# Hybrid encoder trunk on one core: last part of the down projection in written order, merge units reordered, second multiplier transposed later

## The chip, the core and the metric

The kernel runs on one core of a Trainium2 chip. The metric is device time in microseconds for the whole program, both layers. PE is TensorE's matmul stream, PEld its weight loads, DVE is VectorE, ACT is ScalarE, POOL is GpSimd; SP issues most of the DMAs.

## The reference, cut to what matters

A trunk of two layers on 256 positions by 1024 channels, all in float32. Each layer is

```
h = rmsnorm(x, norm1_g) * (1 + sc1) + sh1
x = x + g1 * token_mix(h)          # Fourier branch and retention branch, merged by gates
h = rmsnorm(x, norm2_g) * (1 + sc2) + sh2
x = x + g2 * conv_ffn(h)           # up projection, conv, gelu gate, down projection
```

and a last rmsnorm follows. The six vectors sh, sc, g come from one conditioning vector times `ada_w` (1024 x 6144 in each layer). In `token_mix` the two branch results are merged as `sigmoid(a_f) * y_f + sigmoid(a_r) * y_r`, where a_f and a_r are projections of h, y_f is the Fourier branch times `w_fourier` and y_r is the retention branch times `w_ret`.

## The kernel before, in words

**Precision by splitting.** Each float32 operand is held as a high part and a remainder: `split` (L60) has ACT write the rounded copy (L61) and DVE the difference (L62). Each product is then three matmuls: high by high, and the two mixed ones (`mm_xs` L138, `mm_ws` L144).

**Weights.** `plan` (L75 to L96) lists all weight blocks of 1 MB in the order of use. `ahead` loads a block into one of four `raw` buffers by SP and splits it into two halves, each in a `wt` buffer (four of them, so two blocks) or, for some, in a general buffer (`wb`). `nextw` takes the next block and prepares the one after. A buffer is free again only when its last reader is done, so a load on SP or a split on ACT may wait for that.

**Conditioning.** `ada_dots` (L194) loads 1 MB of `ada_w` into a `raw` buffer and makes two dot products on DVE (L184). They fill gaps: `side` issues a few in each stage, and `pl` says which. A finished multiplier column (`gc`) is turned into a row by a PE transpose, an ACT copy and two DMAs from POOL's queue (`rows`, L214 to L221).

**Order.** The code is traced in the order written; a scheduler then sets the order on every engine by its own estimate of what is ready first, and each engine runs its list in that order. `later(n, fn)` and `tick` (L123, L126) place a small piece of work n steps further on in the trace.

**Merge** (L588 to L622). Four column blocks c; for each, four units of 48 matmuls (`mm_w`): z = 0 and 1 are the gate projections of h (tile `hT`), z = 2 the Fourier branch (`yf`), z = 3 the retention branch (`yrT`). The last head's attention runs among the units of c = 0, and its normed result is transposed (L598) and split into the second half of `yrT`, which the unit z = 3 of c = 0 reads.

**FFN.** After the output projection and the second norm come 22 tiles of the up projection (three of them in another layout, their transposes at L686), each with convolution and gate. The down projection keeps four accumulators, two row blocks m of 128 positions by two column blocks z of 512 (in the last layer the second row block has columns of 512, 256 and 256), and walks through 11 weight blocks. For the first 7 it does all four accumulators at each block; the last SK = 4 blocks (`ws`: two in `wt`, two in `wb`) are all prepared first, and then each accumulator is finished in turn (L725 to L732). After each column follow the residual (rt L735, c_xs L736), and squares for the next norm (L738); `norm_mod` (L268) then makes 1/rms on POOL (L232), scales (xn, L242 on DVE and L244 on ACT), and a few ticks later transposes (L251) and modulates (hm, L262 and L264) and splits into `hT`, which the first projection of the next layer reads.

## Time and profile before

| what | value |
|---|---|
| median of 3 runs | 897.24 us (893.81 to 897.34) |
| profiled execution, its own time | 897.42 us |
| its span, first to last instruction | 895.6 us |
| PE busy, matmuls | 98%, 6250 |
| DVE busy, ACT busy | 82%, 56% |
| mean granted TensorE clock | 0.992 |
| bytes by DMA, mean rate | 210.85 MB, 235 GB/s |

Busy shares are means over the whole span; busy PE is modelled from the size of each matmul, so that matmuls in a row overlap. What matters here is where PE's list stands still, and on which instruction of another engine. The profiled execution lies 0.18 us above the median of the runs, and 1.86 us of its time lie outside the span.

### The profile page before, as it was taken

To read this page: it belongs to the slowest core of one execution; us is meant where nothing else is said; L and a number is where in the kernel's file an instruction comes from. 1 tells how busy PE (TensorE), PEld (TensorE's weight loads), DVE (VectorE), ACT (ScalarE), POOL (GpSimd) and SP (SyncE) were. 2 spreads that over 40 slices of the span, in tenths; PEclk is the share of its full clock that TensorE was granted. 3 is DMA by queue.
4 is the path that set the end of the run, shared out by engine and by line. 5 is a ranking of instruction groups with operands and counts; after the bars stand their busy time and mean duration, and the time that the engine had idled before them with its cause. 6 is when DMAs were issued, how large, how long until landed. Compare 5 with 4: busy or idle time off the path is not lost.

```text
span 895.6 us, 15358 instructions
## 1 busy us (share of the span) xinstructions
PE 874.5 (98%) x6250; PEld 816.1 (91%) x6250; DVE 735.7 (82%) x1135; ACT 500.7 (56%) x736; POOL 23.0 (3%) x33
## 2 busy tenths in 40 slices
PE   7999999899999999999989999999999999999996
PEld 5889999899989999998878899999998999999885
DVE  6899999788885999899687879997777769999563
ACT  5666446344465876763474545554444767677441
POOL 1000000000000000000000000010000000000000
PEclk9999999999999999999999999999999999999999
DMA  8995665878884356579755666657778444655521
GB/s 322 378 348 201 236 236 194 300 295 299 311 336 145 142 190 209 199 257 407 291 188 188 249 245 223 253 194 261 280 272 324 171 165 165 210 207 195 188 95 48
DMA packets 33033, 210.85 MB, mean 235 GB/s; under 512 B 4001, under 2 KB 4289, under 8 KB 10178
## 3 DMA queue, kind: packets, MB, share of 16 engines
q1 hardware_dynamic: 31682, 207.16, 63.3%
q0 software_dynamic: 704, 2.11, 0.7%
q8 instruction: 49, 0.80, 0.3%
q10 hardware_dynamic: 576, 0.59, 0.2%
q14 instruction: 22, 0.18, 0.1%
HBM read 208.79 MB, written 1.06 MB: 234 GB/s over the span
## 4 chain that ended last, share of the span: by engine, by line
PE 83%; DVE 9%; DMA 3%; issue 2%; ACT 2%; POOL 1%; POOLq 0%; SPq 0%; ACTq 0%
PE ps L148 48%; PE ps L141 11%; PE ps L140 11%; PE ps L142 11%; DVE wt L62 3%; DMA raw<-in_ada_dram 2%; DVE raw L184 2%; PE ps L251 1%; DMA raw<-in_wx_dram 1%; PE ps L463 1%; DVE qk L62 1%; ACT wt L61 1%; DVE rc L501 0%; DVE rsn L502 0%; DVE yrT L62 0%
## 5 line engine op out<-in xcount | busy, mean ns | idle before, releaser
L148 PE MATMUL ps<-hT,wt 128*128 128x256 f32 x3368 | 392.1, 277 | 0.0
L148 PEld LDWEIGHTS ps<-hT,wt 128*128 128x128 f32 x3368 | 388.2, 188 | 0.4
L62 DVE TENSOR_TENSOR wt<-raw,wt 128x1024 fp32r<-128x1024 f32 (+1 forms) x270 | 325.8, 1214 | 72.3 <-ACT wt L61 70.8
L61 ACT ACTIVATE wt<-raw 128x1024 fp32r<-128x1024 f32 (+1 forms) x270 | 282.2, 1052 | 175.8 <-PE ps L148 84.5
L184 DVE CUSTOM_DVE_ANT_0 raw<-raw,c_cbc,c_adab 128x1024 f32<-128x1024 f32 x96 | 121.2, 1280 | 9.7 <-DMA raw<-in_ada_dram 9.5
L140 PE MATMUL ps<-wt,hT 128*128 128x512 f32 (+1 forms) x240 | 84.1, 367 | 4.8 <-ACT hT L61 2.5
L141 PE MATMUL ps<-wt,hT 128*128 128x512 f32 (+1 forms) x240 | 87.8, 366 | 0.0
L142 PE MATMUL ps<-wt,hT 128*128 128x512 f32 (+1 forms) x240 | 87.8, 367 | 0.0
L647 ACT ACTIVATE cv<-ps,c_cvw 128x256 f32<-128x256 f32 x88 | 49.4, 561 | 29.6 <-PE ps L148 17.9
L141 PE MATMUL ps<-wt,act 128*128 128x512 f32 (+1 forms) x162 | 59.3, 367 | 0.0
L142 PE MATMUL ps<-wt,act 128*128 128x512 f32 (+1 forms) x162 | 59.2, 366 | 0.0
L140 PE MATMUL ps<-wt,act 128*128 128x512 f32 (+1 forms) x162 | 58.7, 366 | 0.0
L140 PEld LDWEIGHTS ps<-wt,hT 128*128 128x128 f32 x240 | 45.4, 190 | 13.3 <-ACT hT L61 3.4
L142 PEld LDWEIGHTS ps<-wt,hT 128*128 128x128 f32 x240 | 46.1, 192 | 7.6
L141 PEld LDWEIGHTS ps<-wt,hT 128*128 128x128 f32 x240 | 46.0, 192 | 6.9
L148 PE MATMUL ps<-yrT,wt 128*128 128x256 f32 x384 | 49.0, 288 | 3.0 <-DVE yrT L62 3.0
L148 PEld LDWEIGHTS ps<-yrT,wt 128*128 128x128 f32 x384 | 47.5, 195 | 3.5 <-DVE yrT L62 3.3
L148 PE MATMUL ps<-yf,wt 128*128 128x256 f32 x384 | 46.5, 281 | 0.0
L648 DVE SCALAR_TENSOR_TENSOR cv<-ps,c_cvw,cv 128x255 f32<-128x255 f32 x88 | 41.1, 479 | 6.3 <-ACT cv L647 6.1
L148 PEld LDWEIGHTS ps<-yf,wt 128*128 128x128 f32 x384 | 45.8, 189 | 0.0
L651 DVE SCALAR_TENSOR_TENSOR cv<-ps,c_cvw,cv 128x255 f32<-128x255 f32 x88 | 41.2, 480 | 1.6
L141 PEld LDWEIGHTS ps<-wt,act 128*128 128x128 f32 x162 | 30.6, 189 | 5.2 <-DVE wt L62 0.3
(154 smaller groups left out, 940.5 us busy)
## 6 DMA issues: line engine op xcount, KB each, us to landing
raw<-in_ww_dram SPq DMA_DIRECT2D x48, 1024.0 KB, 5.5
raw<-in_ada_dram SPq DMA_DIRECT2D x40, 1024.0 KB, 4.9
raw<-in_up_dram SPq DMA_DIRECT2D x38, 1024.0 KB, 4.8
raw<-in_wx_dram SPq DMA_DIRECT2D x24, 1024.0 KB, 6.6
raw<-in_down_dram SPq DMA_DIRECT2D x22, 1024.0 KB, 4.8
raw<-in_ada_dram SPq DMA_DIRECT2D x16, 512.0 KB, 7.4
raw<-in_wx_dram SPq DMA_DIRECT2D x16, 512.0 KB, 6.9
raw<-in_upx_dram SPq DMA_DIRECT2D x6, 1024.0 KB, 7.3
```

The lines of the kernel that those rows point to most:

```text
L61: A.activation(dst_h, src if hi_src is None else hi_src, AF.Copy)
L62: V.tensor_tensor(out=dst_l, in0=src, in1=dst_h.bitcast(F32), op=ALU.subtract)
L140: T.matmul(pt, xh, wh, start=start, stop=False)
L141: T.matmul(pt, xh, wl, start=False, stop=False)
L142: T.matmul(pt, xl, wh, start=False, stop=stop)
L148: T.matmul(pt[:, z], w, x[:, z], start=start and i == 0, stop=stop and i == 2)
L184: V.tensor_tensor_reduce(out=wb, in0=wb, in1=cbc, scale=1.0, scalar=adab[:, l, v * KT + k : v * KT + k + 1], op0=ALU.mult, op1=ALU.add, ac ...
L251: T.transpose(pt[:, b * P : (b + 1) * P], xn[:, b * P : (b + 1) * P], ident)
L463: T.matmul(pt, dfc[:, x, part, :], pq[i][:, y, :, o : o + P], start=(j == 0), stop=(j == 2))
L647: A.activation(o, pt, AF.Identity, scale=cvw[:, l, 1, c : c + 1], bias=cvw[:, l, 3, c : c + 1])
L648: V.scalar_tensor_tensor(out=o[:, 1:], in0=pt[:, : S - 1], scalar=cvw[:, l, 0, c : c + 1], in1=o[:, 1:], op0=ALU.mult, op1=ALU.add)
L651: V.scalar_tensor_tensor(out=o[:, : S - 1], in0=pt[:, 1:], scalar=cvw[:, l, 2, c : c + 1], in1=o[:, : S - 1], op0=ALU.mult, op1=ALU.add)
```

## The change

Four edits:

1. **Merge.** The 16 units are named by a table `MERGE` of (c, z). The unit z = 3 of c = 0, the first reader of `yrT`, now comes after (1, 0), the first gate projection of the next column block. The plan of weights follows the table. The conditioning loads of a column block are still issued after its unit z = 3, so they are traced one unit later for c = 0.
2. **Down projection, last part.** PE follows the written order from the last four weight blocks on to the end of the loop (`manual_schedule`). Row block m = 0 is finished before m = 1, and within a row block the weight block is the outer loop and the column the inner one (but for the second row block of the last layer). The norm's transposes come 2 ticks later for m = 0 (after 24 matmuls of m = 1) and 3 for m = 1.
3. **Weight splits behind the modulation.** When the first norm's modulation of m = 0 for the next layer has been traced, weight splits after the first two halves are issued behind its split on ACT and DVE (`hold`, `issue_after`), until the next layer has its first four blocks.
4. **Second multiplier.** `rows` for g2 no longer comes at the end of the merge; it is kept in `behind` and issued after the third transposed FFN tile.

```
+MERGE = [(0, 0), (0, 1), (0, 2), (1, 0), (0, 3), (1, 1), (1, 2), (1, 3)] + [(c, z) for c in (2, 3) for z in range(4)]
...
     def split(dst_h, dst_l, src, hi_src=None):
-        A.activation(dst_h, src if hi_src is None else hi_src, AF.Copy)
-        V.tensor_tensor(out=dst_l, in0=src, in1=dst_h.bitcast(F32), op=ALU.subtract)
+        h = A.activation(dst_h, src if hi_src is None else hi_src, AF.Copy)
+        l = V.tensor_tensor(out=dst_l, in0=src, in1=dst_h.bitcast(F32), op=ALU.subtract)
+        return h.ins, l.ins
...
-        for c in range(4):
-            plan += [(w_[8 + 4 * z + c], 0, 64) for z in range(4)]
+        plan += [(w_[8 + 4 * z + c], 0, 64) for c, z in MERGE]
...
-                split(t[:, 0, :], t[:, 1, :], w[:, c * 1024 : (c + 1) * 1024])
+                with ExitStack() as order:
+                    for ins in hold[1:] if hold and hold[0] <= 0 else ():
+                        order.enter_context(tc.issue_after(ins))
+                    split(t[:, 0, :], t[:, 1, :], w[:, c * 1024 : (c + 1) * 1024])
+                if hold:
+                    hold[0] -= 1
...
-        later(2, rows)
+        if i == 0:
+            later(2, rows)
+        else:
+            behind.append(rows)
...
+        def mod(hf):
+            made = modulate(l, i, m, hf, norm_t(xns[hf]), hp[hf])
+            if i == m == 0:
+                hold[:] = [2, *made]
...
             wu = [nextw(3 - i) for i in range(4)]
+            hold.clear()
...
+        for c, z in MERGE:
+            pt = ps()
+            mm_w(pt, (hp, hp, yfp, yrp)[z], nextw(), 0 if (c, z) == (1, 1) else None)
+            if z < 2:
+                t = sig[c, z] = tmp("sig")
                 A.activation(t, pt, AF.Sigmoid)
+                continue
+            t = sig[c, z - 2]
+            V.tensor_tensor(out=t, in0=pt, in1=t, op=ALU.mult)
+            if z == 2:
+                continue
+            y, t = sig.pop((c, 0)), sig.pop((c, 1))
+            V.tensor_tensor(out=y, in0=y, in1=t, op=ALU.add)
             o = mp[c // 2][:, :, 2 * (c % 2) : 2 * (c % 2) + 2, :]
+            split(o[:, 0], o[:, 1], y.rearrange("p (b t) -> p b t", b=2))
             side("c", (len(pl["c"]) + 3 - c) // (4 - c))
...
         for j in range(NX):
             later(2 * j + 1, lambda j=j: t_gated(j))
+        while behind:
+            later(2 * NX - 1, behind.pop())
...
+        end = ExitStack()
+        end.enter_context(tc.manual_schedule(engines={mybir.EngineType.PE}))
         for m in range(2):
...
+            n = len(cols[m])
+            if m == 1 and last:
+                order = [(i, z) for z in range(n) for i in range(SK)]
+            else:
+                order = [(i, z) for i in range(SK - 1) for z in range(n)] + [(SK - 1, z) for z in range(n)]
+            for x, (i, z) in enumerate(order):
+                for kk in range(2):
+                    down(ws[i], NT - SK + i, m, z, kk)
+                if i == SK - 1:
+                    column(z)
+                if x % 2 == 1:
+                    tick()
...
-                norm_mod(l + 1, 0, m, hp, ss, 3, 3)
+                norm_mod(l + 1, 0, m, hp, ss, 2 + m, 2 + m)
```

What moves on the engines is seen at three places. In all of these rows ps is an accumulator in PSUM; line numbers are those of the kernel they are from, and L148 before is L157 now, L62 is L64, L184 is L193.

PE in the merge of the first layer, before: yf is the Fourier unit of c = 0, gpart holds the retention result, whose transposes are the x8 row.

```order
L148 MATMUL ps<-yf,wt 128x256 x48
L598 MATMUL ps<-c_ident,gpart 128x128 x8
L148 MATMUL ps<-yrT,wt 128x256 x13
L148 MATMUL ps<-hT,wt 128x256
L148 MATMUL ps<-hT,wt 128x128 x3
L148 MATMUL ps<-yrT,wt 128x256 x35
```

and now:

```order
L157 MATMUL ps<-yf,wt 128x256 x48
L613 MATMUL ps<-c_ident,gpart 128x128 x8
L157 MATMUL ps<-hT,wt 128x256 x48
L157 MATMUL ps<-yrT,wt 128x256 x48
L157 MATMUL ps<-hT,wt 128x256
```

A whole gate unit of 48 matmuls now stands between the transposes and the first matmul on `yrT`.

DVE at the same place, now: ag and vr are the statistics of the last head, nb the bias for its norm, the ISA rows with raw are conditioning dot products, sig is the merge's multiply.

```order
L552 BN_AGGR ag<-bs 128x2 x2
L193 ISA raw,sct<-raw,c_cbc,c_adab 128x1024
L193 ISA sct 128x1
L554 TENSOR_SCALAR vr<-ag 128x2
...
L558 SCALAR_TENSOR_TENSOR nb<-ag,rr 128x2
L64 TENSOR_TENSOR wt<-raw,wt 128x1024
L565 TENSOR_TENSOR gpart<-yn,gpart 128x256 x2
...
L632 TENSOR_TENSOR sig<-ps,sig 128x512
L193 ISA raw,c_sh_98<-raw,c_cbc,c_adab 128x1024
L193 ISA c_sh_98 128x1
L64 TENSOR_TENSOR yrT<-ps,yrT 128x4x128 x2
```

Before, these first two dots (sct) stood ahead of the statistics, the c_sh dots around nb and the gc dots ahead of the `yrT` split; each of them now stands one place later. The rows left out are the second sct dot behind vr, and one row of sc and one weight split behind gpart.

DVE at the layer boundary, now, from the first row block's scaled half (xn) on: rt and c_xs are the residual of the second row block, wt and wb weight splits of the next layer's first four blocks.

```order
L254 TENSOR_SCALAR xn<-c_xs,rs 128x512
L64 TENSOR_TENSOR wt<-raw,wt 128x1024 x2
L276 TENSOR_SCALAR hm<-ps,c_sc_103,c_sh_99 128x128 x4
L64 TENSOR_TENSOR hT<-hm,hT 128x4x128 x2
L64 TENSOR_TENSOR wt<-raw,wt 128x1024
L754 TENSOR_TENSOR rt<-ps,g_600 128x512
L64 TENSOR_TENSOR wt<-raw,wt 128x1024
L755 TENSOR_TENSOR c_xs<-c_xs,rt 128x512
L64 TENSOR_TENSOR wb<-raw,wb 128x1024
```

and before:

```order
L242 TENSOR_SCALAR xn<-c_xs,rs 128x512
L735 TENSOR_TENSOR rt<-ps,g_600 128x512
L62 TENSOR_TENSOR wt<-raw,wt 128x1024
L736 TENSOR_TENSOR c_xs<-c_xs,rt 128x512
L62 TENSOR_TENSOR wt<-raw,wt 128x1024 x2
L264 TENSOR_SCALAR hm<-ps,c_sc_103,c_sh_99 128x128 x2
L735 TENSOR_TENSOR rt<-ps,g_600 128x512
L264 TENSOR_SCALAR hm<-ps,c_sc_103,c_sh_99 128x128 x2
L736 TENSOR_TENSOR c_xs<-c_xs,rt 128x512
L62 TENSOR_TENSOR hT<-hm,hT 128x4x128 x2
```

The modulation of the first row block now runs in one piece, ahead of the second block's residual and of all but two weight splits. On PE the transposes that feed it had 12 down-projection matmuls behind them before the first use of `hT`; now they have 24.

More of the change, by code (lines that the diff above doesn't have):

```diff
@@ L121, in trunk @@
     waiting = []
+    behind = []
     def later(n, fn):
@@ L272, in norm_mod @@
         for hf, t in ((0, t0), (1, t1)):
-            later(t, lambda hf=hf: modulate(l, i, m, hf, norm_t(xns[hf]), hp[hf]))
+            later(t, lambda hf=hf: mod(hf))
     def tok(m):
@@ new lines, in trunk, with yr_t, last_scores @@
+        yrp = [pair("yrT", [4, S]) for i in range(2)]
+        def yr_t(hf):
+            for m in range(2):
+                pt = ps()
+                for b in range(4):
+                    T.transpose(pt[:, b * P : (b + 1) * P], yr[:, m, hf * 512 + b * P :][:, :P], ident)
+                split(yrp[hf][:, 0, :, tok(m)], yrp[hf][:, 1, :, tok(m)], pt.rearrange("p (b t) -> p b t", b=4))
+        def last_scores():
+            sts[H - 1] = scores(H - 1, qks.pop(H - 1))
+        later(1, last_scores)
@@ new lines, in trunk @@
+        later(2, lambda: yr_t(0))
+        later(3, lambda: attend(H - 1, sts.pop(H - 1)))
+        later(6, lambda: yr_t(1))
+        sig = {}
+        for c, z in MERGE:
[3 more added lines that the diff above has]
+                t = sig[c, z] = tmp("sig")
+                A.activation(t, pt, AF.Sigmoid)
+                continue
[5 more added lines that the diff above has]
+            V.tensor_tensor(out=y, in0=y, in1=t, op=ALU.add)
@@ L620, in trunk @@
             o = mp[c // 2][:, :, 2 * (c % 2) : 2 * (c % 2) + 2, :]
-            split(o[:, 0], o[:, 1], sig[0].rearrange("p (b t) -> p b t", b=2))
+            split(o[:, 0], o[:, 1], y.rearrange("p (b t) -> p b t", b=2))
             side("c", (len(pl["c"]) + 3 - c) // (4 - c))
@@ L724, in trunk, with column @@
             nc.sync.dma_start(fg, a["rowv"].to_broadcast([P, D]))
+        end = ExitStack()
+        end.enter_context(tc.manual_schedule(engines={mybir.EngineType.PE}))
         for m in range(2):
             ss = sp.tile([P, 4], F32, tag="ss", name="ss", bufs=3)
-            for z, (c0, w) in enumerate(cols[m]):
-                for i in range(SK):
-                    for kk in range(2):
-                        down(ws[i], NT - SK + i, m, z, kk)
-                    if i % 2 == 1:
-                        tick()
+            def column(z):
+                c0, w = cols[m][z]
                 cs = slice(c0, c0 + w)
@@ L756, in trunk @@
                     A.dma_start(out[0, tok(m), s], o)
+        end.close()
 def _tables():
```

29 lines of the change are left out of this document (2 added, 27 removed).

## The prediction

> **What bounds the kernel now.** I read the page first, then PE's waits, then the granted clock in stretches around the longest of them, and last the order of time on PE, DVE, ACT and POOL there.
>
> ```profile
> PE 874.5 (98%) x6250; PEld 816.1 (91%) x6250; DVE 735.7 (82%) x1135; ACT 500.7 (56%) x736; POOL 23.0 (3%) x33
> ...
> PE 83%; DVE 9%; DMA 3%; issue 2%; ACT 2%; POOL 1%; POOLq 0%; SPq 0%; ACTq 0%
> ```
>
> PE is the bound: 98% busy, and 83% of the chain that ended last. No edit changes its 6250 matmuls, so what can be won are the moments in which its list stands still. The view of PE's waits (us in total, times, longest) names them:
>
> ```profile
> PE ps L148 <- DVE yrT L62: 3.0, 2, 2.7
> PE ps L140 <- ACT hT L61: 2.5, 2, 2.3
> PE ps L172 <- DMA c_cbc<-in_crow_dram: 2.5, 1, 2.5
> PE ps L140 <- ACT wt L61: 2.3, 1, 2.3
> ```
>
> The third and fourth are at the start, which the change doesn't touch. The first is the merge unit that reads `yrT` (2.7 us in the first layer, 0.3 in the second); the second is the first matmul of layer 2 on `hT`. Each long stop has a second price. Stretches, with busy us and instructions for PE, PEld, DVE, ACT, POOL, then the granted clock, the DMA share and GB/s:
>
> ```profile
> 165.50:171.50 6.00, 3.36 (x27) 3.02 (x26) 5.45 (x9) 2.03 (x3) 0.00 (x0) 1.00 0.97 310
> 171.50:175.00 3.50, 3.46 (x16) 3.46 (x17) 1.12 (x1) 0.66 (x1) 0.00 (x0) 0.51 0.77 281
> 451.00:454.80 3.80, 1.49 (x7) 0.88 (x6) 3.80 (x9) 3.23 (x8) 0.00 (x0) 1.00 0.84 276
> 454.80:458.30 3.50, 3.50 (x10) 2.73 (x10) 3.06 (x5) 3.38 (x5) 1.46 (x1) 0.51 0.27 56
> ```
>
> Right behind each stop the clock is 0.51 for 3.5 us, so 3.5 x 0.49 = 1.7 us more are lost.
>
> [...]
>
> **Merge, first layer.** PE in order of time:
>
> ```profile
> 166.34 1.94 PE L148 MATMUL ps<-yrT,wt 128*128 128x256 f32 x13
> 168.12 0.75 PE L148 MATMUL ps<-hT,wt 128*128 128x256 f32 x4
> 171.54 5.83 PE L148 MATMUL ps<-yrT,wt 128*128 128x256 f32 x35 [2.68 <-DVE yrT L62]
> 177.21 11.23 PE L148 MATMUL ps<-hT,wt 128*128 128x128 f32 x94
> 188.28 5.82 PE L148 MATMUL ps<-yf,wt 128*128 128x256 f32 x48
> 193.93 5.82 PE L148 MATMUL ps<-yrT,wt 128*128 128x256 f32 x48
> ```
>
> From 188.28 to 193.93 a unit of 48 takes 5.65 us, 0.118 each. From 166.34 to 177.21 are 13 + 4 + 35 = 52 matmuls: 6.12 us at that pace, 10.87 taken, so **4.75 us lost** (the stop, the slow clock, and 0.3 of small ones). What was late stands on DVE and POOL:
>
> ```profile
> 158.69 0.76 DVE L533 BATCH_NORM_STATS2 bs<-ps 128x6 f32<-128x256 f32 x2
> 160.02 1.61 POOL L538 TENSOR_TENSOR rr<-vr,c_nhalf 128x2 f32<-128x2 f32 x1 [3.38 <-DVE vr L536]
> 164.08 0.76 DVE L547 TENSOR_TENSOR gpart<-yn,gpart 128x256 f32<-128x256 f32 x2
> 166.05 1.29 DVE L184 CUSTOM_DVE_ANT_0 raw<-raw,c_cbc,c_adab 128x1024 f32<-128x1024 f32 x1 [1.22 <-DMA raw<-in_ada_dram]
> 170.21 1.28 DVE L62 TENSOR_TENSOR yrT<-ps,yrT 128x512 fp32r<-128x512 f32 x2
> ...
> 154.91 0.33 SPq L67 DMA_DIRECT2D raw<-in_ada_dram  x1
> ...
> 157.31 8.72 DMA raw<-in_ada_dram
> ...
> raw<-in_ada_dram SPq DMA_DIRECT2D x40, 1024.0 KB, 4.9
> ```
>
> DVE runs its list in order, and a conditioning dot whose load took 8.72 us (median of its kind 4.9) stood ahead of the split. Now unit (1, 0) runs from 166.34 to 172.0, and the unit on `yrT` reads the second half's remainder after 13 more matmuls, at 173.5. Unchanged, the split would end at 171.5. But the dots move too. The loads are traced one unit later, so the load issued at 154.91, second of three, is now the first; at 4.9 us it lands at 159.8. Its first dot now stands ahead of vr, whose statistics end at 159.7: vr at 161.1 (dot 1.29), POOL 1.61, then the bias, ACT's norm and the two gpart multiplies, about 2 us together: 164.8, just what the two multiplies reach now (164.08 + 0.76 = 164.84), because the other dot ran ahead of the weight split there. The second load, issued when the first one's buffer comes free (two dots, 162.3), lands at 167.2, its dot ends at 168.5, and the two splits at 169.8: 3.7 us ahead of need. Gain 4.75, bounds 0 (as late as before, or a new stop of the same price) and 4.75. I take 4.6. The weights of (1, 0) and (0, 3) only swap places in the same four `wt` buffers.
>
> **Merge, second layer.**
>
> ```profile
> 605.45 1.94 PE L148 MATMUL ps<-yrT,wt 128*128 128x256 f32 x13
> 607.23 0.96 PE L148 MATMUL ps<-hT,wt 128*128 128x256 f32 x7
> 608.49 4.39 PE L148 MATMUL ps<-yrT,wt 128*128 128x256 f32 x35 [0.30 <-DVE yrT L62]
> 612.72 10.88 PE L148 MATMUL ps<-hT,wt 128*128 128x256 f32 x91
> ```
>
> 55 matmuls take 7.27 us against 55 x 0.118 = 6.47: **0.8 us lost**, no slow clock. The need moves back by 5.65 us, and ahead of the split stand as many dots as before, two. Gain 0.8, bounds 0 and 0.8.
>
> **Layer boundary.**
>
> ```profile
> 430.03 0.39 PE L140 MATMUL ps<-wt,act 128*128 128x512 f32 x1
> ...
> 443.36 0.68 DVE L735 TENSOR_TENSOR rt<-ps,g 128x512 f32<-128x512 f32 x1
> 446.89 0.71 ACT L244 ACTIVATE xn<-c_xs,rs 128x512 f32<-128x512 f32 x1
> 447.72 1.03 PE L251 MATMUL ps<-c_ident,xn 128*128 128x128 f32 x8
> 451.10 0.39 PE L142 MATMUL ps<-wb,act 128*128 128x512 f32 x1
> 451.44 0.73 DVE L264 TENSOR_SCALAR hm<-ps,c_sc,c_sh 128x128 f32<-128x128 f32 x2
> 453.80 0.50 PE L140 MATMUL ps<-wt,hT 128*128 128x512 f32 x1 [2.31 <-ACT hT L61]
> 453.91 1.30 DVE L62 TENSOR_TENSOR hT<-hm,hT 128x512 fp32r<-128x512 f32 x2
> 455.41 1.46 POOL L232 TENSOR_TENSOR rs<-ss,c_nhalf 128x1 f32<-128x1 f32 x1 [9.01 <-DVE ss L230]
> 458.95 0.39 PE L140 MATMUL ps<-wt,hT 128*128 128x512 f32 x1
> ...
> L62 DVE TENSOR_TENSOR wt<-raw,wt 128x1024 fp32r<-128x1024 f32 (+1 forms) x270 | 325.8, 1214 | 72.3 <-ACT wt L61 70.8
> ```
>
> From 430.03 to 447.72 are 78 matmuls, 0.227 each. The last down matmul starts at 451.10 and is through at 451.33; 15 matmuls on `hT` follow up to 458.95, which need 3.4 us and take 7.62: **4.2 us lost**. The cause is the order: transposes at 447.72, with only 12 matmuls (2.7 us) behind them.
>
> The new order ends the last down matmul at the same 451.33, since the matmuls are the same. Row block 1 then fills 48 x 0.227 + 0.8 of transposes = 11.7 us, so row block 0 is through at 439.6, and its transposes stand after 24 matmuls, at 445.1. From the second column's rt to the end of xn the trace takes 443.36 to 447.60 = 4.2 us; from 439.9 that gives 444.1, so PE doesn't stop at the transposes (1.0 us to spare). They end at 445.9. The modulation and splits then need, in one piece, the four hm and two `hT` rows of DVE (0.7 for a pair, 1.30): by 449, against need at 451.3. If it all took as long as before (447.72 to 453.80, 6.1 us) it would be 451.2, still no stop.
>
> What is late next is row block 1's norm. DVE has, from about 449.0 on, two wt and four wb splits (1.2 each), two rt and two c_xs (0.6 each), ss and xn ahead of the end of that xn: 10.2 us, so 459.2 with ACT and POOL at their short durations, 460.1 with the 1.46 us of POOL above. PE reaches these transposes 36 matmuls (8.2 us) after 451.33, at 459.5. A stop of 0 to 1.0 us; I take 0.5. Each of the six halves of weights held back comes about 2.5 us ahead of its use by the same count. Gain 4.2 - 0.5 = 3.7; bounds 0.2 (a new stop as dear as the old one) and 4.2.
>
> **The rest.** In the last layer's tail PE waits for one weight half once:
>
> ```profile
> 868.02 0.19 PEld L141 LDWEIGHTS ps<-wt,act 128*128 128x128 f32 x1 [0.32 <-DVE wt L62]
> ```
>
> The new order needs that half 6 matmuls later: gain 0.15, bounds 0 and 0.3. The second multiplier's transpose is one matmul on PE wherever it stands; POOL's two DMAs for it now come behind the norm's power instead of ahead of it, and no wait of PE names them: 0. PE would have to stand in front of that transpose for it to cost, and its column is made before the output projection begins.
>
> **Sum.** 4.6 + 0.8 + 3.7 + 0.15 = 9.25 us. The profiled execution took 897.42 (span 895.6 and 1.8 around it), so 888.2; it lies 0.2 above the median of the runs, so I predict **888.0 us**. Own range of this case: 886.0 to 890.5 (up to 2.5 us of new small stops).
>
> **Rivals.**
> - *The merge stop comes back in the first layer.* Now a dot stands ahead of vr. With a load of 8.72 us instead of 4.9, vr, the transposes and all behind them are 3.8 us later; PE stands 3.0 us, plus 1.7 of slow clock: 4.7 us, so 892.7. For it: such a load is in the trace, at this very place. Against it: that load flew beside the multiplier row's broadcast and behind another load, and the one issued at 154.91 landed in time for its dot.
> - *The boundary stop moves to row block 1's transposes.* PE can't pass them, and xn needs 10.2 us of DVE's list behind 449. If the whole list is 2 us later, the stop is 2.5 us and the clock halves: 4.2 instead of 0.5, so 891.7. Against it: 451.2 is the latest the trace gives for `hT`, and DVE then has less in front.
> - *Nothing gained.* Both of the above at once, and no gain in the second layer: 888.0 + 4.7 + 3.7 + 0.8 = 897.2.
> - *Slower.* One mechanism: DVE's list held by the first conditioning load in the merge. Each us that it lands after 160.8 is a us of PE, plus 1.7 in all. To eat the 9.25 us and 4.5 more it must land 12 us after that, an 18 us load: the slowest loads named above took 8.72. Time then from 902 on.
> - *The pieces don't act.* The orders above show that they do; what is unsure is only whether something else was the last to arrive.
>
> **How the numbers follow.** Chances: forecast 0.58, first rival 0.17, second 0.14, nothing gained 0.07, slower 0.04. A change of 0.5%, 4.5 us, is about what a measurement of this kernel can tell from none: below 892.8 is faster. The forecast, the second rival, and half of the first lie there: 0.58 + 0.14 + 0.08 = 0.80; same 0.16; slower 0.04. The range: with all terms at their upper bounds (4.75 + 0.8 + 4.2 + 0.3 = 10.05) the median would be 887.2, and I go 1.4 below that, since one of the three runs before was 3.4 us faster than the other two; above, it takes in both rivals: 885.8 to 893.4.
>
> **What would show it.** Right: PE's waits no longer name `yrT` or the first `hT` with more than 0.5 us; the clock is 1.00 in every stretch after the start; between the transposes of row block 0 and the first `hT` matmul stand 24 down matmuls without idle time; the gpart multiplies end within 1 us of the `yf` unit's end. Wrong: a stretch at 0.51 near 170 or 460; an idle time ahead of L263 (the transposes) above 1 us; a dot with idle time from a DMA ahead of vr. If the time is above 893 though these stops are gone, the lost time has another source than PE's order.

## The result, and the profile after

| | before | changed |
|---|---|---|
| median of the runs side by side (4 each) | 896.38 us (893.81 to 897.34) | 887.57 us (887.22 to 888.77) |
| profiled execution, its span | 897.42, 895.6 us | 888.77, 886.9 us |
| mean granted clock | 0.992 | 0.998 |

The ratio is 0.9904, with a 95% interval of 0.9884 to 0.9924: faster by about 1%. The prediction was 888.0 us. The total came out nearly as forecast; how it came about did not, as the stages below show.

The page of the changed kernel, busy time and the chain that ended last, and its view of PE's waits (us in total, times, longest):

```profile
PE 867.5 (98%) x6250; PEld 809.2 (91%) x6250; DVE 736.7 (83%) x1135; ACT 501.8 (57%) x736; POOL 22.1 (2%) x33
...
PE 75%; DVE 13%; DMA 5%; ACT 3%; issue 3%; POOL 1%; POOLq 0%; SPq 0%; ACTq 0%; DVEq 0%
...
PE ps L149 <- ACT wt L63: 3.9, 2, 2.3
PE ps L150 <- DVE wt L64: 2.3, 2, 1.3
PE ps L149 <- ACT hT L63: 0.2, 1, 0.2
```

The waits on `yrT` and on the first `hT` of layer 2, 2.7 and 2.3 us before, are gone. New are waits on split weights (`wt`): of the first row 1.6 us and of the second all 2.3 us stand at the two output projections. PE's busy time fell by 7.0 us with the same number of matmuls; the two stretches of slow clock, 3.4 us each at a granted clock of 0.50, account for 3.4 of that, and the rest needs another cause. Not all of the waits on weights are new: the second output projection had one of 0.6 us before. And 13% of the chain now run over DVE and 5% over DMA, against 9% and 3%.

**Stages.** From both traces, the time between landmarks on PE: start is the 17th matmul on `hT` (at 19.18 us before and 19.07 now, behind the slow clock of the start: 0.51 from 14.5 to 18.0 us before; matmuls 0.43 us apart up to 16.6 us now, and 0.23 from 17.0 on), T is the second set of transposes ahead of a merge's `yrT` (L598 before, L613 after), W the first matmul of the output projection, N the first transpose of the second norm, F the last transpose of the transposed FFN tiles, D the first down matmul, E the discrete transform of layer 2. In us:

| stage | before | changed | difference | predicted |
|---|---|---|---|---|
| start to T, layer 1 | 146.38 | 146.40 | 0.0 | 0 |
| T to W, merge of layer 1 | 79.28 | 72.27 | -7.0 | -4.6 |
| W to N, output projection | 16.47 | 20.37 | +3.9 | 0 |
| N to D, FFN's up projection | 129.26 | 129.85 | +0.6 | 0 |
| D to E, down projection and boundary | 87.70 | 84.15 | -3.55 | -3.7 |
| E to T, layer 2 | 126.39 | 127.01 | +0.6 | 0 |
| T to W, merge of layer 2 | 75.33 | 71.85 | -3.5 | -0.8 |
| W to N | 17.28 | 17.68 | +0.4 | 0 |
| N to D | 129.26 | 129.75 | +0.5 | 0 |
| D to the end | 69.03 | 68.56 | -0.5 | -0.15 |

The ten differences make -8.5 us. The rows of the FFN's up projection, 129 us long, show how well a stage repeats that no edit means to touch: within 0.6 us.

**The merge of layer 1 went by the prediction's walk.** DVE, POOL and PE of the changed kernel in order of time:

```profile
159.84 1.26 DVE L193 CUSTOM_DVE_ANT_0 raw<-raw,c_cbc,c_adab 128x1024 f32<-128x1024 f32 x1
161.03 0.16 DVE L554 TENSOR_SCALAR vr<-ag 128x2 f32<-128x2 f32 x1
161.34 1.61 POOL L556 TENSOR_TENSOR rr<-vr,c_nhalf 128x2 f32<-128x2 f32 x1 [4.46 <-DVE vr L554]
164.20 0.75 DVE L565 TENSOR_TENSOR gpart<-yn,gpart 128x256 f32<-128x256 f32 x2
167.48 1.28 DVE L193 CUSTOM_DVE_ANT_0 raw<-raw,c_cbc,c_adab 128x1024 f32<-128x1024 f32 x1
168.68 0.69 DVE L64 TENSOR_TENSOR yrT<-ps,yrT 128x512 fp32r<-128x512 f32 x1
...
166.26 5.90 PE L157 MATMUL ps<-hT,wt 128*128 128x256 f32 x48
171.99 5.82 PE L157 MATMUL ps<-yrT,wt 128*128 128x256 f32 x48
177.65 5.85 PE L157 MATMUL ps<-hT,wt 128*128 128x256 f32 x50
183.34 5.60 PE L157 MATMUL ps<-yf,wt 128*128 128x256 f32 x48
188.78 5.60 PE L157 MATMUL ps<-yrT,wt 128*128 128x256 f32 x48
```

A conditioning dot stands ahead of vr, which comes at 161.03 (worked out: 161.1), POOL takes 1.61, the gpart multiplies end at 164.95 (164.8), the dot after them ends at 168.8 (168.5), and the unit on `yrT` at 171.99 has no idle time in front. From T to the next `yf` unit PE now takes 17.88 us (165.46 to 183.34), before 22.72 (165.56 to 188.28): 4.8 us less.

Two things follow that the prediction does not have. Behind the unit at 177.65 a unit of 48 matmuls takes 5.44 us (183.34 to 188.78) and no longer 5.65 (188.28 to 193.93 before). And PE runs into a wall at the output projection, here with ACT, SP's queue and the DVE dots ahead of it:

```profile
230.87 1.29 DVE L193 CUSTOM_DVE_ANT_0 raw<-raw,c_cbc,c_adab 128x1024 f32<-128x1024 f32 x1 [2.56 <-DMA raw<-in_ada_dram]
233.33 0.33 SPq L70 DMA_DIRECT2D raw<-in_ada_dram  x1
234.53 5.68 SPq L70 DMA_DIRECT2D raw<-in_wx_dram  x3
241.15 2.00 ACT L63 ACTIVATE wt<-raw 128x1024 fp32r<-128x1024 f32 x2 [7.59 <-DMA raw<-in_wx_dram]
242.26 0.49 PE L149 MATMUL ps<-wt,mg 128*128 128x512 f32 x1 [1.61 <-ACT wt L63]
244.06 0.50 PE L150 MATMUL ps<-wt,mg 128*128 128x512 f32 x1 [1.31 <-DVE wt L64]
```

ACT has stood idle for 7.59 us for a block of `wx`, the output projection's weights. SP issued it only at 234.53, behind the last conditioning loads, since a `raw` buffer comes free only when the dots on it are done, and these wait for their own loads. The buffers are not held by dots alone: between 215 and 245 us SP waited 20.7 us for weight splits on DVE and 6.4 us for dots. The groups of dots, of before and then of the changed kernel, show the same: idle time on loads ahead of them has nearly doubled; from T to N of layer 1 it is 6.3 us, before 1.2.

```profile
L184 DVE CUSTOM_DVE_ANT_0 raw<-raw,c_cbc,c_adab 128x1024 f32<-128x1024 f32 x96 | 121.2, 1280 | 9.7 <-DMA raw<-in_ada_dram 9.5
```

```profile
L193 DVE CUSTOM_DVE_ANT_0 raw<-raw,c_cbc,c_adab 128x1024 f32<-128x1024 f32 x96 | 121.2, 1279 | 17.8 <-DMA raw<-in_ada_dram 17.8
```

**The boundary** of the changed kernel, PE, DVE and ACT around the transposes of both row blocks:

```profile
442.38 1.03 PE L263 MATMUL ps<-c_ident,xn 128*128 128x128 f32 x8
445.56 1.29 DVE L64 TENSOR_TENSOR hT<-hm,hT 128x512 fp32r<-128x512 f32 x2 [0.20 <-ACT hT L63]
448.71 0.39 PE L149 MATMUL ps<-wt,hT 128*128 128x512 f32 x1
...
457.44 1.09 PE L263 MATMUL ps<-c_ident,xn 128*128 128x128 f32 x8 [0.41 <-DVE xn L254]
```

The first `hT` matmul starts without a wait, 1.9 us after the split of `hT` ended at 446.85. At row block 1's transposes PE now stands for about 0.6 us, of which the row names 0.41.

### The profile page after: what moved, and what is told of

It reads as the page before. It is cut to its first block, busy times and chain, and to the rows that moved or that the text cites. A ratio compares the mean times of both kernels' runs of the same rounds, so it can differ in the third digit from the quotient of the medians.

```text
span 886.9 us, 15356 instructions
## 1 busy us (share of the span) xinstructions
PE 867.5 (98%) x6250; PEld 809.2 (91%) x6250; DVE 736.7 (83%) x1135; ACT 501.8 (57%) x736; POOL 22.1 (2%) x33
## 4 chain that ended last, share of the span: by engine, by line
PE 75%; DVE 13%; DMA 5%; ACT 3%; issue 3%; POOL 1%; POOLq 0%; SPq 0%; ACTq 0%; DVEq 0%
PE ps L157 41%; PE ps L150 11%; PE ps L149 11%; PE ps L151 11%; DVE wt L64 5%; DMA raw<-in_ada_dram 3%; DVE raw L193 3%; PE ps L263 1%; ACT wt L63 1%; DMA raw<-in_ww_dram 1%; DMA raw<-in_wx_dram 1%; PE ps L481 1%; DVE qk L64 1%; ACT hm L274 1%; DVE sig L632 0%
## 5 line engine op out<-in xcount | busy, mean ns | idle before, releaser
L157 PE MATMUL ps<-hT,wt 128*128 128x256 f32 (+1 forms) x3368 | 390.6, 277 | 0.0
L157 PEld LDWEIGHTS ps<-hT,wt 128*128 128x128 f32 x3368 | 386.6, 188 | 0.4
L64 DVE TENSOR_TENSOR wt<-raw,wt 128x1024 fp32r<-128x1024 f32 (+1 forms) x270 | 325.4, 1214 | 56.3 <-ACT wt L63 55.3
L193 DVE CUSTOM_DVE_ANT_0 raw<-raw,c_cbc,c_adab 128x1024 f32<-128x1024 f32 x96 | 121.2, 1279 | 17.8 <-DMA raw<-in_ada_dram 17.8
L157 PE MATMUL ps<-yf,wt 128*128 128x256 f32 x384 | 45.0, 277 | 0.0
L157 PE MATMUL ps<-yrT,wt 128*128 128x256 f32 x384 | 45.0, 277 | 0.0
L157 PEld LDWEIGHTS ps<-yrT,wt 128*128 128x128 f32 x384 | 44.3, 188 | 0.0
L157 PEld LDWEIGHTS ps<-yf,wt 128*128 128x128 f32 x384 | 44.3, 188 | 0.0
```

Of the source, the lines that this page charges most:

```text
L64: l = V.tensor_tensor(out=dst_l, in0=src, in1=dst_h.bitcast(F32), op=ALU.subtract)
L157: T.matmul(pt[:, z], w, x[:, z], start=start and i == 0, stop=stop and i == 2)
L193: V.tensor_tensor_reduce(out=wb, in0=wb, in1=cbc, scale=1.0, scalar=adab[:, l, v * KT + k : v * KT + k + 1], op0=ALU.mult, op1=ALU.add, ac ...
```

## Experiments

All times are medians beside runs of the kernel before on the same chip; stages are from the profiled execution of each run. "T to N" is merge and output projection of layer 1 together: 95.75 us before, 92.64 changed. There is one profile of each kernel, so how its stages differ from execution to execution is not known.

**1. The first edit alone.**

```
-        for c in range(4):
-            plan += [(w_[8 + 4 * z + c], 0, 64) for z in range(4)]
+        plan += [(w_[8 + 4 * z + c], 0, 64) for c, z in MERGE]
... (the merge loop by MERGE; rows, down projection and splits as before)
```

> The first edit alone on the kernel before: the merge table with its plan of weights, everything else as it was. Theory A (stops alone, as in the prediction): 4.6 + 0.8 = 5.4 us less than before. Theory B (stops, and a second thing that the profile of the changed kernel shows: in the merges 256-column matmuls follow one another every 113.3 ns instead of 117.8 ns once the two 256-column matmuls that are cut into four of 128 columns stand in one piece, worth 2.2 us in each merge; and in the first layer's merge the loads then come late, so that PE stands 3.8 us at the output projection): 5.5 + 2 x 2.2 - 3.8 - 0.4 = 5.7 us less. The total hardly tells them apart, the profile does: A expects 117.8 ns from the cut to the end of the first merge and no stop at the output projection, B 113.3 ns and a stop of about 3.8 us there.

891.58 us against 896.89, ratio 0.9938 (0.9916 to 0.9960): 5.3 us less. B's pace came true in both merges (the 384 matmuls on `yf` take 45.0 us of PE in all, as in the changed kernel, against 46.5 before), and the stop too, with another name and dearer. PE at the end of the merge, in order of time:

```profile
242.10 0.37 PE L225 MATMUL ps<-c_ident,gc 128*8 128x128 f32 x1 [3.88 <-DVE gc L193]
```

PE stands 3.88 us in front of the second multiplier's transpose, whose last dot is late, and the clock is 0.50 for 6.8 us from the middle of this stop on (240.24 to 247.06 us). T to N is 95.19: of the 4.75 us at the `yrT` stop only 0.6 are left in layer 1. The rest of the gain is the second merge (T to W -3.5) and 1.6 us at the layer boundary, which this kernel did not change: its stop of 2.3 us came again, but without the slow clock behind it (1.00 from 455.27 to 458.68 us).

**2. The second and third edits alone.**

```
+        end.enter_context(tc.manual_schedule(engines={mybir.EngineType.PE}))
+                    for ins in hold[1:] if hold and hold[0] <= 0 else ():
+                        order.enter_context(tc.issue_after(ins))
-                norm_mod(l + 1, 0, m, hp, ss, 3, 3)
+                norm_mod(l + 1, 0, m, hp, ss, 2 + m, 2 + m)
```

> The second and third edits alone on the kernel before: the last part of the down projection in written order, and the weight splits behind the modulation. Theory A: the stop of 2.3 us at the first matmul on hT and its slow clock go, a stop of about 1 us at row block 1's transposes comes: 3.6 us less than before. Rival: in the changed kernel the loads ahead of the layer boundary run otherwise because the merge was changed too; then the gain alone is under 2.5 us and the stop at row block 1's transposes is over 1.5 us.

892.76 against 896.89, ratio 0.9958 (0.9939 to 0.9978): 4.1 us less. D to E is 84.09 us, 3.6 less, the same as with the merge changed. Theory A holds; the boundary does not depend on the merge. Its second merge ran 2.7 us faster (72.65 us from T to W), all pace, though no line of it was changed; the 384 matmuls on `yf` of both layers take 45.9 us, 46.5 before.

**3. The changed kernel without the cut.** In the merge one product's second and third matmul are each cut into two of 128 columns (`cut` in `mm_w`).

```
-            mm_w(pt, (hp, hp, yfp, yrp)[z], nextw(), 0 if (c, z) == (1, 1) else None)
+            mm_w(pt, (hp, hp, yfp, yrp)[z], nextw(), None)
```

> The changed kernel without the cut in the merge: all 256-column matmuls of the merge go whole. Theory A (pace has another source than the cut): the same time as the changed kernel, 113.3 ns in both merges. Theory B (the cut in one piece flips the pace): in the first layer's merge 117.8 ns up to the output projection, which PE reaches 2.2 us later; most of that is taken back, since its stop there shrinks from 3.8 to about 1.6 us or less (with a stop that short the slow clock may not come, 1.7 us more). In the second layer's merge the pace is 113.3 ns already from unit (1, 0) on, ahead of the cut, so nothing is lost there. In all within 2 us of the changed kernel, to either side.

889.98 against 896.89, ratio 0.9922 (0.9902 to 0.9942). PE behind the place of the cut:

```profile
184.86 5.82 PE L157 MATMUL ps<-yf,wt 128*128 128x256 f32 x48
190.51 5.82 PE L157 MATMUL ps<-yrT,wt 128*128 128x256 f32 x48
```

Without the cut 5.65 us from unit to unit up to the output projection, with it 5.44: B. T to W is 2.1 us longer, W to N 0.9 shorter; of the pace gained in layer 1 so much was given back at the wall. In layer 2 the pace was the fast one without the cut too: of the 45.7 us of the 384 matmuls on `yrT`, 23.3 are layer 1 (four units of 5.82 us), so 22.4 are layer 2, as in the changed kernel; 23.8 before.

**4. The kernel before without its cut.**

```
-                mm_w(pt, hp, nextw(), 0 if c == 1 and z == 0 else None)
+                mm_w(pt, hp, nextw(), None)
```

> The kernel before without the cut in its merges; all 256-column matmuls go whole. In the kernel before the pace went from 113.3 to 117.8 ns just at that cut, in both layers. Theory (the cut toggles between the two paces, so that it helped the changed kernel and hurt the one before): the first layer's merge runs at 113.3 ns from the end of the slow clock on, some 574 matmuls by 4.5 ns, 2.6 us less; in the second layer as much less, if the cut and not the stop of 0.3 us beside it made the pace slow: 2.6 to 5.2 us less in all. Rival (other things set the pace, and the cut's place is chance): 117.8 ns as before, no difference.

891.12 against 894.86, ratio 0.9950 (0.9924 to 0.9977): 3.7 us less by leaving out a cut. PE behind its stop on `yrT`:

```profile
171.91 4.24 PE L148 MATMUL ps<-yrT,wt 128*128 128x256 f32 x35 [2.06 <-DVE yrT L62]
...
186.18 5.60 PE L148 MATMUL ps<-yf,wt 128*128 128x256 f32 x48
191.62 5.60 PE L148 MATMUL ps<-yrT,wt 128*128 128x256 f32 x48
```

5.44 us from unit to unit; in layer 2 T to W is 71.99 us, 75.33 before. In the kernel before itself the 19 matmuls between the end of the slow clock (175.0) and the last half-width matmul of the cut (177.2) already went at 113.4 ns, those behind it at 117.8. So in layer 1 the pace turns at the cut, to slow before and to fast in the changed kernel. But a cut does not turn whichever pace was there: in layer 2 of the changed kernel the pace is the fast one ahead of the cut product, which is in the unit at 610.88, and behind it.

```profile
605.44 5.60 PE L157 MATMUL ps<-yrT,wt 128*128 128x256 f32 x48
610.88 5.84 PE L157 MATMUL ps<-hT,wt 128*128 128x256 f32 x50
616.55 5.60 PE L157 MATMUL ps<-yf,wt 128*128 128x256 f32 x48
621.99 5.60 PE L157 MATMUL ps<-yrT,wt 128*128 128x256 f32 x48
```

T to N is 91.05, less than in the changed kernel, though the stop on `yrT` is still there; no slow clock follows it here (1.00 from 167.36 to 177.60 us), which is worth 1.7 us. The output projection in this kernel starts with a stop of 0.27 us only. This fits a reading that is not shown by itself: with twelve conditioning units in this merge, a stop taken away ahead of the output projection comes back in front of it.

**5. The changed kernel without the fourth edit.**

```
-        if i == 0:
-            later(2, rows)
-        else:
-            behind.append(rows)
+        later(2, rows)
```

> The changed kernel without its fourth edit: the second multiplier's transpose at the end of the merge again, as before. Prediction's pricing: 0. Theory from the run with the first edit alone, where PE stood 3.9 us in front of that transpose and the clock halved behind it: the stretch from the transposes of gpart to the second norm gets 2.5 us longer (92.6 to 95.2 us), and the whole as much. Rival (the load of the last unit, not the transpose, is what both wait for): the stop only changes its name, the stretch stays at 92.6 within 0.5 us.

889.60 against 894.86, ratio 0.9939 (0.9918 to 0.9961). PE ahead of the output projection:

```profile
243.60 0.37 PE L225 MATMUL ps<-c_ident,gc 128*8 128x128 f32 x1 [3.57 <-DVE gc L193]
```

T to N is 95.07, 2.4 longer than with the edit, with half speed for 6.8 us as in experiment 1 (the output projection's matmuls start 0.43 us apart from 244.20 to 248.90 us, and 0.23 behind). The fourth edit was priced at 0 and is worth 2.4 us in this execution, once the first edit is there. All of it is slow clock: 6.8 us at half speed lose 3.4, so without them the stretch would be 1 us shorter than with the edit. The intervals of the two totals overlap (the changed kernel's is 0.9884 to 0.9924), so the gain is shown in the stage and not in the time.

**6. The fourth edit alone.**

```
+            behind.append(rows)
...
+        while behind:
+            later(2 * NX - 1, behind.pop())
```

> The fourth edit alone on the kernel before: the second multiplier's transpose behind the third transposed FFN tile. Prediction: 0, since no wait of PE names that transpose in the kernel before; every stage within 0.3 us but for the chance of the pace and of the clock's halving. Rival: POOL's two DMAs, which now come behind the norm's power, make the norm earlier and the stage with it by 0.5 us.

895.66 against 895.95, ratio 0.9996 (0.9976 to 1.0015): nothing in the time, as predicted for it alone. Its stages did not stay as they were. T to W of layer 1 is 77.80 us (79.28 before) and that of layer 2 72.64 (75.33), both at the fast pace behind the cut, with the order of units and the cut of the kernel before; W to N of layer 1 is 19.82 (16.47), with stops of 0.66, 0.76 and 0.41 us on split weights. PE behind the cut of layer 1:

```profile
189.61 5.60 PE L158 MATMUL ps<-yf,wt 128*128 128x256 f32 x48
195.05 5.60 PE L158 MATMUL ps<-yrT,wt 128*128 128x256 f32 x48
```

So the fast pace comes without the first edit too, and the output projection is late here as well, though the stop on `yrT` still stands ahead of it. Experiments 5 and 6 together say that the price of this edit hangs on the first one, as far as one profile of each can.

**7. The changed kernel without the third edit.**

```
-            if i == m == 0:
-                hold[:] = [2, *made]
```

> The changed kernel without its third edit: weight splits are not held behind the modulation of row block 0. Theory: the splits of the next layer's weights, ready earlier, stand ahead of the modulation on DVE and ACT, each 1.2 us, so hT comes 1 to 4 us later and PE stops at the first matmul on it; the boundary stage (84.15 us from the down projection to the discrete transform) gets 0.5 to 4 us longer. Rival: the scheduler puts the modulation first by itself, since its inputs are ready as early; then 84.1 us as with the edit.

887.95 against 894.86, ratio 0.9913 (0.9885 to 0.9941). D to E is 83.73 us, 0.4 less than with the edit, and the first `hT` matmul has no wait. The rival holds: the scheduler puts the modulation first by itself, and holding the splits back is worth nothing here. The stop of 0.4 us at row block 1's transposes is gone too; the second kernel without the edit, the last one below, has the same 83.73 us, and the eight kernels with both the second and the third edit have 84.05 to 84.15.

**8 to 12: what makes the wall.** Four kernels move conditioning units out of the merge of layer 1 or to another place in it; a fifth joins two of them.

*Four units (second multiplier) to FFN tiles 7, 9, 11, 13:*

```
-            pl = dict(v=[], h=G1, c=[z[i] for i in range(4) for z in (SC, SH, G2)], d=NX1)
+            pl = dict(v=[], h=G1, c=[z[i] for i in range(4) for z in (SC, SH)], d=NX1, f=G2)
...
+            if j >= 7 and j % 2:
+                side("f", 1)
```

> The changed kernel with four of the twelve conditioning units of the first layer's merge (those of the second multiplier) moved to the FFN tiles 7, 9, 11 and 13, so that the merge loads 4 MB less. Theory B (the loads bound the first layer's merge once PE is faster there): the stop of 3.8 us at the output projection goes, and the whole is 3 to 4 us faster than the changed kernel, if the eight dots that now stand among the FFN tiles are hidden under PE. Rival (the stop there comes from the order on ACT and DVE and not from the loads): the stop stays, and the time is the same within 1 us. Second rival: the dots are in the way among the FFN tiles, where DVE has the convolutions: the stop goes, but the FFN gives 1 to 3 us back.

890.22 against 896.89, ratio 0.9930 (0.9908 to 0.9952). T to N is 88.80, 3.8 us less: the wall is gone. But the FFN's tiles are 4.1 us longer (94.30 against 90.22 from F to D), for PE waits there on splits behind the dots:

```profile
327.91 2.27 PE L157 MATMUL ps<-hT,wt 128*128 128x256 f32 x17 [1.37 <-DVE wt L64]
```

The theory is right about the stop and the second rival about the FFN, at a higher price than its 1 to 3 us; the sum is nothing.

*Two units behind the second norm:*

```
+            pl = dict(... for z in (SC, SH, G2) if z is not G2 or i < 2], d=NX1, f=G2[2:])
...
                 if m == 1:
                     ahead((j + 1) // 2)
+                    side("f", 1)
```

> The changed kernel with two of the twelve conditioning units of the first layer's merge (the last two of the second multiplier) moved behind the second norm, among the three transposed FFN tiles, where DVE stood idle for about 9 us between 275 and 295 in the changed kernel. Theory (the loads and dots of the merge bound PE at the output projection, and the full DVE list bounds what can be moved among the later FFN tiles): the merge up to the output projection's end gets 3 to 4 us shorter as with four units moved, and the FFN keeps its length within 0.5 us instead of getting 4.2 us longer; so 3 to 4 us less than the changed kernel. Rival (two units are not enough): half of the stop stays, 1.5 to 2 us less. Rival (the dots stand in the way of the splits there too): the FFN stage gets 1 to 2 us longer.

890.94 against 894.86, ratio 0.9953 (0.9923 to 0.9982): a miss on both counts. T to N is 94.00, the wall still there; and the scheduler put the dots ahead of the norm's scaling, so that the stretch N to F is 2.9 us longer. In both stretches 3.4 us of slow clock (0.50 from 245.89 us on; from 273.19 us on, with matmuls of 256 columns 0.21 us apart, and 0.12 behind) make 1.7 us of it:

```profile
270.90 1.28 DVE L193 CUSTOM_DVE_ANT_0 raw<-raw,c_cbc,c_adab 128x1024 f32<-128x1024 f32 x1
272.63 0.49 DVE L254 TENSOR_SCALAR xn<-c_xs,rs 128x512 f32<-128x512 f32 x1 [0.44 <-POOL rs L244]
```

```profile
273.17 1.97 PE L263 MATMUL ps<-c_ident,xn 128*128 128x128 f32 x8 [1.97 <-DVE xn L254]
```

*Three units there, their dots held behind the norm's last modulation:*

```
+            pl = dict(... for z in (SC, SH)] + G2[:1], d=NX1, f=G2[1:])
...
+            for ins in late:
+                order.enter_context(tc.issue_after(ins))
```

> The changed kernel with three of the second multiplier's four conditioning units moved out of the first layer's merge to the row block 1 of the transposed FFN tiles, and their dots held behind the last modulation of the second norm on DVE (nine units stay in the merge, 3, 2, 2 and 2 to the column blocks). Theory (in the run with two units moved the dots were put ahead of the second norm's scaling, and two units were too few for the merge): from the transposes of gpart to the second norm 88.8 to 90 us instead of 92.6, the stretch from there to the transposed FFN tiles within 0.7 us of 39.1 to 39.6; 2.5 to 4 us less than the changed kernel. Rival (the merge needs four units out): stop of 1 to 2 us left, so 1 to 2 us less. Rival (DVE has no 8 us to spare before the FFN tiles): the FFN stages get 1 to 3 us longer and eat the gain.

888.57 against 895.95, ratio 0.9916 (0.9893 to 0.9939). N to F is 39.13 us, not longer any more: the units fit there. T to N is 92.30, not the 88.8 to 90 expected: nine units in the merge are hardly better than twelve here, where eight were few enough above. The first rival is right about the stops, which are 0.94 and 1.57 us.

*All twelve units in the merge, but none behind the last column block (4, 4, 4, 0; layer 2: 3, 3, 2, 0):*

```
-            side("c", (len(pl["c"]) + 3 - c) // (4 - c))
+            side("c", (len(pl["c"]) + 2 - c) // (3 - c) if c < 3 else 0)
```

> The changed kernel with the merge's conditioning units behind its first three column blocks only (4, 4, 4, 0 instead of 3 each in the first layer; 3, 3, 2, 0 instead of 2 each in the second), so that the four blocks of the output projection's weights are loaded in a row. Theory (what delays the output projection is the place of the last units' loads ahead of its weights, which take raw buffers until their dots are done): the stop of 3.8 us in the first layer shrinks to under 2 us and that of 1.3 us in the second goes, 2 to 4 us less than the changed kernel. Rival (the amount is what counts: 28 MB in the stretch, whatever the order): the stop moves into the merge's last two column blocks or stays, the time is that of the changed kernel within 1 us.

893.81 against 896.91, ratio 0.9961 (0.9942 to 0.9981): slower than the changed kernel. W to N is 16.35, the stop at the output projection is gone, but T to W is 9.5 us longer than in the changed kernel. The rival is right about the place, for the stops went into the merge, and wrong about the time; half speed behind both stops (0.50 from 202.81 to 206.22 us; 23 matmuls in 4.49 us from 229.69 on, where a unit of 48 takes 5.60) adds 3.4 us:

```profile
203.33 6.84 PE L157 MATMUL ps<-hT,wt 128*128 128x256 f32 x46 [1.64 <-DVE wt L64]
...
229.69 4.49 PE L157 MATMUL ps<-hT,wt 128*128 128x256 f32 x23 [1.26 <-DVE wt L64]
```

*Both: nine units at 3, 3, 3, 0, three late, and no third edit:*

> As the run before it in this set, but also with three of the second multiplier's units behind the second norm as in the earlier run with late units (3, 3, 3, 0 in the first layer), and without the third edit, which the run without it showed to be worth nothing. Theory (place and amount both): no stop at either output projection, from the transposes of gpart to the second norm 88.7 us instead of 92.6, the second layer's output projection 16.5 instead of 17.7; 4 to 5 us less than the changed kernel. Rival (amount only): the stop goes in the first layer alone if nine units are few enough, 3 to 4 us less; if it stays above 2 us here, neither place nor amount of these units is its cause.

887.23 against 896.91, ratio 0.9893 (0.9857 to 0.9929). The stages of its profiled execution: T to N 89.96 (one stop of 1.0 us left), N to F 39.13, D to E 83.73, the second output projection 16.82; its span is 4.4 us shorter than the changed kernel's, about what was expected. Against the run with late units the place (none behind the last column block) is worth 2.3 us of T to N; with eight units against twelve above, that makes place and amount both count, as far as one profile of each can show it. That execution took 884.37 us, but the other three 885.84, 888.62 and 890.85. The interval holds the changed kernel's ratio of 0.9904, so that this version is faster is not shown; only its stages are.

## Why the prediction was right, and where it was not

**In short.** The forecast for what happens at the two places where the stops were is right to about 0.2 us (4.6 against 4.8, 3.7 against 3.55). The sum is right by luck: two things that it does not contain, about 5 us of faster pace in the merges and about 6 us of new stops and slower pace elsewhere, nearly cancel.

- *Merge, first layer, 4.6 us.* The step itself holds: the stop and its slow clock are gone, 4.8 us at that place. (Three of the 52 matmuls counted at 0.118 us are of half width; the first two of them start 58 ns apart, the third 245 ns later.) As a gain of the kernel it fails. The bounds were 0 and 4.75 for that stop only, and the step ended there: it did not ask whether what comes behind, weights and conditioning loads, could keep up with a PE that comes that much sooner. They could not (ACT idle 7.59 us on a load, PE 1.61 and 1.31 us). T to N gained 3.1 us in the changed kernel, with 2.3 us of pace in it; with the first edit alone 0.6. No slow clock followed the new stops: the 3.4 us with the first of them had 1.82 us of PE work, and 3.4 us with 1.80 in another kernel were followed by half clock.
- *Merge, second layer, 0.8 us.* T to W is 3.5 us shorter. The stop is gone as forecast, the other 2.7 us are pace; 0.4 us come back at the output projection. That the first edit brought this pace is not shown: experiments 2, 4 and 6 ran this merge in the old order and at the fast pace (72.65, 71.99 and 72.64 us).
- *The pace.* "0.118 each" was taken as the cost of such a matmul, and the two paces were not seen, though they stand in the trace of before too. The term that is missing is some 530 matmuls in the first merge and 600 in the second, by 4.5 ns each. Experiments 3 and 4 show that the cut of a product, whose place the first edit moved and which the prediction does not mention, decides it in layer 1 of these two kernels. Experiment 6, with the cut at its old place and the fast pace behind it, shows that the place alone does not.
- *Layer boundary, 3.7 us.* Measured 3.55 and, alone, 3.6. The new stop at row block 1's transposes was taken as 0.5 and is about 0.6; it comes with the third edit, for the two kernels that lack this edit do not have it. The price of 4.2 for the old stop holds for the execution profiled; 1.7 of it did not come in experiment 1, which had the same stop.
- *Fourth edit, 0.* Right alone (experiment 6), wrong in company: 2.4 us in the profile of experiment 5. The prediction named the condition, PE standing in front of that transpose, and excluded it because the column "is made before the output projection begins". That was read from the time of PE before the change; with PE 7 us earlier the column was not made.
- *Third edit.* The prediction gave it no price of its own; the stage is 0.4 us shorter without it.
- *Tail, 0.15.* Measured about 0.5, and 0.3 to 0.5 in the other kernels that have the second edit.
- *Rivals.* Neither merge stop nor boundary stop came back at its place. The mechanism of the slower case, DVE's list held by loads, was the right one at the wrong place: it did not bite at vr but 80 us later, at the end of the same merge.
- *Of what would show it*: the clock is at 1.00 in every stretch after the start up to the last 3 us, and the 24 down matmuls stand without idle time, as said. "If the time is above 893 though these stops are gone, the lost time has another source": the time was below 893, and there was another source all the same. A test on the total alone would have missed both.

## What to carry to other kernels

A stop that is taken away makes everything behind it early by as much, so follow the queues (here buffers, loads and dots) to the next place where PE needs them before the gain is booked; here, with twelve units of side loads in one stage, each stop taken away was followed by another one further on. Compare stages between landmarks and not only totals: a total that agrees can be two errors of opposite sign. And price an edit in the company in which it comes: one that was worth nothing alone was worth 2.4 us of a stage with its neighbour, in one profile of each.

## What the runs showed of the hardware

**The granted clock, in steps of 3.413 us.** In the kernel before, the stretches at full clock behind the start last 45, 82 and 127 times 3.413 us, and the two at half clock between them 3.413 us each. In the changed kernel the one stretch at full clock lasts 254 times as long, and with the first edit alone the half clock behind the stop at the output projection lasts twice 3.413 us. Divided into windows of 3.413 us whose edges are these changes (columns as in the prediction), the kernel before at its two stops:

```profile
168.12:171.54 3.42, 0.74 (x5) 0.49 (x4) 3.42 (x7) 0.00 (x0) 0.00 (x0) 1.00 0.88 331
171.54:174.95 3.41, 3.41 (x16) 3.41 (x17) 1.08 (x1) 0.60 (x1) 0.00 (x0) 0.50 0.77 283
451.43:454.84 3.41, 1.09 (x5) 0.85 (x5) 3.41 (x9) 2.84 (x8) 0.00 (x0) 1.00 0.88 295
454.84:458.26 3.42, 3.42 (x10) 2.65 (x10) 2.98 (x5) 3.30 (x5) 1.46 (x1) 0.50 0.27 57
```

the kernel before without its cut, where the same stop on `yrT`, 2.06 us long, falls into two windows, and its stop of 2.3 us on `hT` into one:

```profile
167.36:170.77 3.41, 2.48 (x20) 2.19 (x19) 3.41 (x7) 1.34 (x3) 0.00 (x0) 1.00 0.90 308
170.77:174.18 3.41, 2.27 (x20) 2.27 (x21) 2.21 (x3) 0.67 (x1) 0.00 (x0) 1.00 1.01 356
174.18:177.60 3.42, 3.42 (x33) 3.42 (x32) 2.61 (x4) 1.46 (x2) 0.00 (x0) 1.00 0.90 328
447.25:450.66 3.41, 1.10 (x5) 0.59 (x4) 3.41 (x8) 2.84 (x6) 0.00 (x0) 1.00 0.91 293
450.66:454.08 3.42, 3.42 (x10) 2.67 (x9) 2.98 (x6) 3.29 (x6) 1.46 (x1) 0.50 0.29 55
```

the first edit alone, the window with most of the boundary stop and the one behind it:

```profile
451.86:455.27 3.41, 1.90 (x8) 1.58 (x9) 3.41 (x8) 2.98 (x7) 0.29 (x1) 1.00 0.64 247
455.27:458.68 3.41, 3.41 (x16) 2.81 (x16) 2.96 (x4) 3.29 (x5) 1.18 (x1) 1.00 0.49 120
```

and the two of nearly equal busy time, two units moved and the changed kernel:

```profile
242.47:245.89 3.42, 1.80 (x7) 1.27 (x8) 3.36 (x5) 3.33 (x4) 0.00 (x0) 1.00 0.39 120
245.89:249.30 3.41, 3.41 (x10) 2.63 (x9) 3.25 (x4) 0.00 (x0) 0.00 (x0) 0.50 0.90 372
```

```profile
238.83:242.25 3.42, 1.82 (x8) 1.15 (x7) 3.42 (x7) 1.10 (x2) 0.00 (x0) 1.00 0.98 362
242.25:245.66 3.41, 2.09 (x7) 1.24 (x7) 3.41 (x7) 2.73 (x4) 0.00 (x0) 1.00 1.01 413
```

The first number after the width is PE's busy time in the window. Six windows at full clock with PE busy for 0.74 to 1.80 us were followed by one at half clock: the four of them above, one with 1.40 us ahead of the output projection with the first edit alone (236.82 to 240.24) and one with 1.22 us with all twelve units behind three column blocks (199.39 to 202.81). Four with 1.82 us (the changed kernel), 1.85 (three late units, 245.16 to 248.58), 1.90 (the first edit alone) and 1.94 (no third edit, 239.66 to 243.07) were followed by one at full clock. In the case of 1.80 us PE stood still for about 1.6 of the 3.4 us. One window in the last 10 us does not go with these: in the kernel with two units moved, from 880.77 on, it had 1.71 us and was followed by one at full clock, and why is not known. Of the five stops of 2.0 to 2.7 us named here, three (2.68, 2.31 and 2.3 us, the last in the kernel before without its cut) had half clock behind them, which cost 1.7 us more than their length, and two (2.06 us there, 2.3 us with the first edit alone) had not: the price of 1.7 us that the prediction put on each stop is one that a stop of this size paid only sometimes.

**Two paces of the same matmul.** In the merges a 256-column matmul, each with its own weights, starts 113.3 or 117.8 ns after the one before it, in stretches of tens of microseconds, with the clock at 1.00 in both (units of 48 in 5.44 and 5.65 us above). At the products cut into half-width matmuls the mean times between starts, ahead and behind, were:

| kernel, layer | half-width matmuls | ahead | behind |
|---|---|---|---|
| before, 1 | three from 168.24 us on, the fourth at 177.21 | 113.4 ns (19 ahead of the fourth) | 117.8 ns |
| before, 2 | four in a row from 607.34 us on | 113.4 ns (8) | 117.8 ns, behind a stop of 0.30 us |
| changed, 1 | four in a row from 177.76 us on | 117.8 ns | 113.4 ns |
| changed, 2 | four in a row from 610.99 us on | 113.3 ns | 113.4 ns |

So the pace turned at the cut in both directions, and once it did not turn. It also changed where nothing is cut: in the changed kernel from 117.8 to 113.3 ns across the eight transposes at 270.23 us. Outside the merges (N to D, E to T and N to D) 347 more matmuls of the changed kernel went at the slow pace than before (668 against 321, with 2073 against 2420 at the fast one), which is 1.6 us. What the two paces are inside PE no run shows; and whether they explain that stretches which no edit touches, such as the start to T (145.9 to 147.2 us), differ between kernels was not tested.
